# Output projection: gates and turns of rows 0 and 1 placed inside the mLSTM's last head, its own head in a fixed order

## The chip, the cores and the metric

One core of one Trainium2 chip runs the kernel. The metric is the device time of one launch in microseconds, median of three runs. The engines in the profile are PE (TensorE: matmuls, transposes by a matmul with the identity), DVE (VectorE), ACT (ScalarE), POOL (GpSimd) and SP, which only issues DMAs; ACT and POOL issue some DMAs too, in line with their other instructions.

## What is computed

A hybrid encoder block on x of 2048 x 1024 in float32. Its mixing part has two groups of 512 channels, an mLSTM with 4 heads in both directions and a Hyena operator; each is normalised and both go through one output projection. An MLP follows.

```python
y_m = group_rms(h_m, M_HEADS, mlstm_norm_w)        # h_m = (h_fwd + h_bwd) * o_gate
...
z = cv[..., OFF_HX2:OFF_HX2 + H_WIDTH] * two_sided_fft_conv(z, filt[:, 0, 1], filt[:, 1, 1], fb[1])
y_h = group_rms(z, H_GROUPS, hyena_norm_w)
mix = jnp.concatenate([y_m, y_h], axis=-1).astype(x.dtype) @ w_out
x = x + rms_norm(mix, norm_mix_post)
hm = rms_norm(x, norm_mlp_pre)
ff = jnp.square(jax.nn.relu(hm @ w_mlp_in)) @ w_mlp_out
x = x + rms_norm(ff, norm_mlp_post)
```

## The kernel before

The stages run one after the other with overlaps: input projection beside the filters, Hyena's long convolution, the mLSTM, the output projection, the MLP.

**Who orders what.** Tile pools hand out buffers by tag; a scheduler puts the instructions of each engine into one fixed order, by the order of the program and by when it reckons that operands and buffers are there. Inside `tc.manual_schedule(engines=...)` the engines named keep the order in which the code emits; where such a region falls among instructions from outside, and the order of engines not named (SP and POOL here), stay the scheduler's. On the chip each engine goes through its order and waits where something isn't ready. A DMA issued by ACT stands in ACT's order.

**The mLSTM** (`mlstm`, line 881) counts n from 0 to 68: 4 heads of 16 chunks. At each n `scores` (PE scores, ACT Exp on the mask tile mb) runs for chunk n, `values` (line 999) for chunk n - 5, and `issue` runs what values left for later: ACT's scalings into nm, DVE's sums, and for every fourth chunk the quotients (DVE's reciprocal into den, then on POOL the product nm and the sum ht) and the store of ht into ym, which ACT issues (L234). At n = 50 to 59 `loads_ahead` emits the loads that the output projection needs first. At n = 61, 64 and 68 `first_gate` does row 0's gate in three steps: the product of the inverse transform's matmuls (`gated`, L1290 and L1291) with the gate data xg; its `group_norm` (Square on ACT L1295, reduction on DVE L1297, Sqrt on ACT L239, reciprocal on DVE L241, product on POOL L1300); and `turn_split` (four PE transposes L1306, ACT's high part L166, DVE's low part L169).

**The output projection** (`out_proj`, line 1319) works on 16 rows of 128 positions. Operands are split into a high and a low part, and `mm3` makes each product of three matmuls (lines 159 to 161): low x high, high x low, high x high. `part(po, e, y, k0)` does half e of the 1024 columns for four of eight k blocks, 12 matmuls. The first half of a row by k (k0 = 4) takes the Hyena group, from `gate` and `turned`; the second (k0 = 0) the mLSTM group, from `mixed` (loads of ym and the gate o, a POOL product L1371, group_norm) and `turned`. `weight(k)` makes the parts of block k: ACT's high (L1342), DVE's low (L1343). Ahead of the loop over rows `out_proj` is not in a manual region: weights 4 to 7 with gate 1, row 0's first half, row 1's turn and first half, row 0's mixed operand, weights 0 to 3. The loop (L1455) is a manual region for PE, DVE and ACT for each i; at i it turns row i + 1's Hyena operand, does row i's first half, gate i + 3, row i + 1's mixed turn, and row i's second half. Tag xg has two buffers for gate data and o together, tag tp three PSUM banks for gates and turns, tag po three and tag h1 two for the sums.

Of the kernel before, what the change touches and what calls it, by code (L numbers as in the profile page):

```python
# [147 lines left out]
class Builder:  # L148
# [95 lines left out]
    def build(self):  # L244
        tc, nc = self.tc, self.nc
        with ExitStack() as c:
# [57 lines left out]
            self.ahead["y"] = [op.tile([128, 4, 128], F32R, name=f"y0{e}") for e in range(2)]  # L304
# [11 lines left out]
            for _ in range(6):  # L316
                next(out)
# [563 lines left out]
    def mlstm(self):  # L881
        LAG, AHEAD = 5, 10
        LOADS = {1: "v1", 5: "q1", 9: "k2", 14: "v2", 19: "q2", 32: "k3", 32 + LAG: "v3", 40: "q3"}
        self.later = []
# [6 lines left out]
        for n in range(64 + LAG):  # L891
# [19 lines left out]
            if 50 <= n < 60:  # L911
                self.loads_ahead(n - 50)
            if n in (61, 64, 64 + LAG - 1):
                self.first_gate((61, 64, 64 + LAG - 1).index(n))
# [354 lines left out]
    def loads_ahead(self, i):  # L1269

        ahead, tile = self.ahead, self.mearly.tile
        if i == 0:
            self.gate_loads(0, *ahead["gate", 0])
        elif i < 5:
            self.load(ahead[3 + i], self.io["w_out"][128 * (3 + i):128 * (4 + i), :])
        elif i == 5:
# [4 lines left out]
            t = tile([128, 3, 512], F32, tag="v", name="rda")  # L1281
            ahead["gate", 1] = t[:, 0:2], t[:, 2]
            self.gate_loads(1, *ahead["gate", 1])
# [25 lines left out]
    def first_gate(self, step):  # L1309

        (rd, xg), y = self.ahead["gate", 0], self.ahead["y"]
# [7 lines left out]
    def out_proj(self, c):  # L1319
# [24 lines left out]

        def gate(h):
            if h == 1:
                rd, xg = ahead.pop(("gate", 1))
            else:
                rd = scratch("rd").rearrange("p (r c) -> p r c", r=2)
                xg = wk.tile([128, 512], F32, tag="xg", name="xg", bufs=2)  # L1350
                self.gate_loads(h, rd, xg)
# [14 lines left out]
        def mixed(h):  # L1366
            yt = wk.tile([128, 512], F32, tag="ym", name="ymt")
            ot = wk.tile([128, 512], F32, tag="xg", name="ot", bufs=2)
            for dst, ap in ((yt, self.ym), (ot, self.vo[:, 512:1024])):
                self.load(dst, self.rows(ap, h))  # L1370
            pool.tensor_tensor(yt, yt, ot, ALU.mult)  # L1371
# [3 lines left out]
        def part(po, e, y, k0):  # L1375
            cs = slice(512 * e, 512 * e + 512)
            for k in range(4):
# [55 lines left out]
        zs, pos, yz = {}, {}, {0: ahead["y"]}  # L1433
        for k in (4, 5, 6, 7):
            weight(k)
            if k == 5:
                zs[1] = gate(1)
            yield
        pos[0] = banks(0)
        for e in range(2):  # L1440
            part(pos[0], e, yz[0], 4)
        yield
        yz[1] = turned(zs.pop(1), 1, 0)
        pos[1] = banks(1)
# [3 lines left out]
        for k in range(4):  # L1448
            weight(k)
# [5 lines left out]
        for i in range(18):  # L1455
            with tc.manual_schedule(engines={mybir.EngineType.PE,mybir.EngineType.DVE,mybir.EngineType.Activation}):
# [17 lines left out]
                if 0 < i < 16:  # L1474
# [4 lines left out]
                    if i > 1:  # L1479
                        part(pos[i], 1, yz[i], 4)  # L1480
# [486 lines left out]
```

## Time and profile before

| | us |
|---|---|
| median of 3 runs | 2704.43 (2702.84 to 2706.27) |
| profiled execution | 2700.58 |
| its span | 2698.5 |
| PE busy | 2598.6 |
| DVE busy | 1541.0 |
| ACT busy | 1230.1 |
| POOL busy | 1206.1 |

The change lies between about 1140 and 1230 us of the span. In a timeline each row has start, duration, engine, line, operation, output and input tiles, shape and count; in brackets the engine's idle time in front of it and who ended it. Matmul ends are modelled, so the distance between starts is the better measure. In a table of stretches, the granted clock of PE (PEclk) is 1.00 at 2.4 GHz and 0.50 at 1.2 GHz.

### The profile page before, as it was taken

How to read it: one execution, taken by the hardware profiler on the slowest of the kernel's cores; microseconds unless marked ns; L12 is line 12 of the kernel's file. 1: busy time of each engine (PE TensorE's matmuls, PEld its weight loads, DVE VectorE, ACT ScalarE, POOL GpSimd, SP SyncE). 2: the span in 40 equal slices, each digit the busy share in tenths (PEclk: the TensorE clock that was granted, in tenths of full speed). 3: DMA queues.
4: the chain of work that ended last, by engine and by line, in shares of the span. 5: the costliest groups of instructions: out<-in, count | busy, mean ns of one | idle time of the engine just before them, and what ended most of it. 6: DMA issues, size and time to landing. Idle time of an engine off the chain costs nothing.

```text
span 2698.5 us, 35390 instructions
## 1 busy us (share of the span) xinstructions
PE 2598.6 (96%) x12237; PEld 2109.2 (78%) x12237; DVE 1541.0 (57%) x2454; ACT 1230.1 (46%) x2292; POOL 1206.1 (45%) x964
## 2 busy tenths in 40 slices
PE   6999999999999998879997999999999999999998
PEld 4778888777798888757774788868888888888876
DVE  5676653777556666656556444474444433543477
ACT  6355544555544446643334444454544333232344
POOL 1211114555225543456667877687772340301232
PEclk9999999999999999899999999999999999999999
DMA  6233336666676658546755444555447453445555
GB/s 173 56 93 110 113 117 216 187 196 187 198 237 180 197 167 272 183 152 213 245 186 210 156 141 163 185 190 172 144 156 282 146 181 98 129 144 160 183 168 214
DMA packets 288354, 465.74 MB, mean 173 GB/s; under 512 B 37542, under 2 KB 149414, under 8 KB 287152
## 3 DMA queue, kind: packets, MB, share of 16 engines
q1 hardware_dynamic: 227600, 324.85, 39.0%
q10 hardware_dynamic: 53264, 117.53, 11.4%
q0 software_dynamic: 7312, 21.11, 3.1%
q8 instruction: 97, 1.59, 0.2%
q14 instruction: 81, 0.66, 0.1%
HBM read 289.27 MB, written 174.13 MB: 172 GB/s over the span
## 4 chain that ended last, share of the span: by engine, by line
PE 39%; DVE 4%; POOL 4%; issue 3%; DMA 2%; ACT 2%; ACTq 0%; DVEq 0%; SPq 0%; POOLq 0%
PE pm L159 13%; PE pm L160 13%; PE pm L161 13%; DMA m<-in_w_mlp_out_dram 1%; POOL xt L1255 1%; DVE cb L169 1%; POOL cb L169 1%; ACT xo L1395 1%; DVE hm L1892 0%; DVE hm L169 0%; DVE xo L1398 0%; DMA hm<-ht 0%; DVE gss L1297 0%; POOL ht L1430 0%; DVE hm L1822 0%
## 5 line engine op out<-in xcount | busy, mean ns | idle before, releaser
L166 ACT CAST cb<-m 128x1024 fp32r<-128x1024 f32 (+1 forms) x342 | 277.4, 846 | 441.3 <-PE pm L159 386.2
L169 DVE TENSOR_TENSOR cb<-m,cb 128x1024 fp32r<-128x1024 f32 (+1 forms) x222 | 237.3, 1106 | 303.1 <-ACT cb L166 302.6
L160 PE MATMUL pm<-cb 128*128 128x512 f32 x880 | 343.4, 390 | 7.8 <-DVE cb L169 7.8
L159 PE MATMUL pm<-cb 128*128 128x512 f32 x880 | 342.3, 389 | 1.3 <-DVE cb L169 1.0
L159 PE MATMUL pm<-hm,cb 128*128 128x512 f32 x840 | 331.4, 394 | 12.3 <-DVE m L1703 6.4
L161 PE MATMUL pm<-cb 128*128 128x512 f32 x880 | 342.5, 389 | 0.0
L160 PE MATMUL pm<-hm,cb 128*128 128x512 f32 x840 | 330.2, 393 | 2.5 <-POOL hm L169 2.5
L161 PE MATMUL pm<-hm,cb 128*128 128x512 f32 x840 | 329.7, 393 | 0.0
L169 POOL TENSOR_TENSOR cb<-m,cb 128x1024 fp32r<-128x1024 f32 x120 | 266.1, 2230 | 57.5 <-ACT cb L166 57.5
L1703 DVE TENSOR_TENSOR m<-pm,m 128x512 f32<-128x512 f32 x224 | 153.9, 690 | 229.4 <-PE pm L161 220.5
L159 PE MATMUL pt<-hn,w 128*128 128x512 f32 x640 | 269.5, 421 | 1.0 <-ACT hn L486 0.9
L160 PE MATMUL pt<-hn,w 128*128 128x512 f32 x640 | 253.9, 397 | 0.7 <-DVE hn L487 0.7
L161 PE MATMUL pt<-hn,w 128*128 128x512 f32 x640 | 253.0, 395 | 0.0
L169 POOL TENSOR_TENSOR raw<-raw,hi 128x512 fp32r<-128x512 f32 x160 | 206.1, 1301 | 99.7 <-ACT hi L166 74.8
L160 PEld LDWEIGHTS pm<-cb 128*128 128x128 f32 x880 | 165.2, 188 | 45.7 <-DVE cb L169 11.7
L159 PEld LDWEIGHTS pm<-hm,cb 128*128 128x128 f32 x840 | 159.2, 189 | 49.0 <-POOL cb L169 7.6
L159 PEld LDWEIGHTS pm<-cb 128*128 128x128 f32 x880 | 165.1, 188 | 36.5 <-ACT junk L1877 1.4
L161 PEld LDWEIGHTS pm<-cb 128*128 128x128 f32 x880 | 165.2, 188 | 33.9
L160 PEld LDWEIGHTS pm<-hm,cb 128*128 128x128 f32 x840 | 159.4, 190 | 37.4 <-POOL hm L169 2.9
L161 PEld LDWEIGHTS pm<-hm,cb 128*128 128x128 f32 x840 | 159.2, 190 | 34.2
L1707 ACT ACTIVATE m<-m 128x512 f32<-128x512 f32 x128 | 80.7, 630 | 229.1 <-DVE m L1703 221.7
L635 POOL DMA_DIRECT2D vp<-vst x96 | 61.2, 642 | 231.7 <-ACT vst L631 230.6
(320 smaller groups left out, 5725.6 us busy)
## 6 DMA issues: line engine op xcount, KB each, us to landing
ga<-m ACTq DMA_DIRECT2D x96, 512.0 KB, 3.6
m<-ga SPq DMA_DIRECT2D x96, 512.0 KB, 3.8
d<-st ACTq DMA_DIRECT2D x64, 512.0 KB, 3.2
m<-in_w_mlp_in_dram SPq DMA_DIRECT2D x64, 512.0 KB, 5.7
m<-in_w_mlp_out_dram SPq DMA_DIRECT2D x114, 256.0 KB, 4.0
raw<-d SPq DMA_DIRECT2D x96, 256.0 KB, 2.9
xt<-in_x_dram SPq DMA_DIRECT2D x32, 512.0 KB, 3.9
dk<-kst SPq DMA_DIRECT2D x32, 512.0 KB, 4.0
```

The lines of the kernel that those rows point to most:

```text
L159: pe.matmul(ps, w[1], x[0], start=first, stop=False)
L160: pe.matmul(ps, w[0], x[1], start=False, stop=False)
L161: pe.matmul(ps, w[0], x[0], start=False, stop=last)
L166: self.act.copy(hi, src)
L169: (eng_lo or self.dve).tensor_tensor(lo, src, hi.bitcast(F32), ALU.subtract)
L635: pool.dma_start(dst[:, 8 * b + e:8 * b + 8:2, cc:cc + 128], st[64 * e:64 * e + 64])
L1255: eng.tensor_tensor(res[:, cs], tmp[e], res[:, cs], ALU.add)
L1395: act.activation(x1, xt, AF.Square, accum_out=ss1[:, h:h + 1])
L1703: dve.tensor_tensor(dst, a, b, ALU.add)
L1707: act.activation(g, g, AF.Relu)
```

## The change

Row 1 gets operand tiles of its own, and its gate data are loaded right behind row 0's. `loads_ahead` starts at n = 40 instead of 50. Six steps of `first_gate` for rows 0 and 1 come at n = 50, 52, 54, 56, 58 and 60. The head of `out_proj` becomes one manual region for PE, DVE and ACT: gate 2's and row 0's mixed loads are emitted first; weights 4 to 7 follow, each with the 12 matmuls of rows 0 and 1 that use it; gate 2 stands behind weight 5; then weights 0 and 1, row 2's turn into row 0's tiles, weights 2 and 3, row 2's first half (its banks from h1 and tp), row 0's mixed operand. In the loop gate 2, row 2's first turn and its first half are gone from i = 0, 1 and 2.

```diff
@@ -301,7 +301,7 @@
             op = self.op = late.enter_context(tc.tile_pool(name="opre", bufs=1, side="right", reuse_waits="tile"))
             self.ahead = {k: op.tile([128, D], F32, name=f"wf{k}") for k in range(4, 8)}
             self.ahead["gate", 0] = op.tile([128, 2, 512], F32, name="rd0"), op.tile([128, 512], F32, name="xg0")
-            self.ahead["y"] = [op.tile([128, 4, 128], F32R, name=f"y0{e}") for e in range(2)]
+            self.ahead["y"] = [[op.tile([128, 4, 128], F32R, name=f"y{r}{e}") for e in range(2)] for r in range(2)]
             self.mtail = late.enter_context(tc.tile_pool(name="mtail", bufs=2, side="right", reuse_waits="tile"))
             self.mwk = ms.enter_context(tc.tile_pool(name="mwk", bufs=2, reuse_waits="tile"))
             self.mps = ms.enter_context(tc.tile_pool(name="mps", bufs=5, space=PSUM, reuse_waits="tile"))
@@ -313,8 +313,7 @@
             self.hq = c.enter_context(tc.tile_pool(name="hmq", bufs=1, reuse_waits="tile"))
             self.hm_pool = {i: self.hq for i in range(3, 8)}
             out = self.out_proj(oc)
-            for _ in range(6):
-                next(out)
+            next(out)
             late.close()
             early.close()
             hp = c.enter_context(tc.tile_pool(name="hmp", bufs=1, side="right", reuse_waits="tile"))
@@ -881,6 +880,7 @@
     def mlstm(self):
         LAG, AHEAD = 5, 10
         LOADS = {1: "v1", 5: "q1", 9: "k2", 14: "v2", 19: "q2", 32: "k3", 32 + LAG: "v3", 40: "q3"}
+        GATES = {50: (0, 0), 52: (0, 1), 54: (1, 0), 56: (1, 1), 58: (0, 2), 60: (1, 2)}
         self.later = []
         for ready in range(AHEAD // 4):
             self.weights(0, ready)
@@ -908,10 +908,10 @@
                 self.state_step(h + 1, steps[1])
             if n in LOADS:
                 self.head_loads(int(LOADS[n][1]), LOADS[n][0])
-            if 50 <= n < 60:
-                self.loads_ahead(n - 50)
-            if n in (61, 64, 64 + LAG - 1):
-                self.first_gate((61, 64, 64 + LAG - 1).index(n))
+            if 40 <= n < 50:
+                self.loads_ahead(n - 40)
+            if n in GATES:
+                self.first_gate(*GATES[n])
             self.issue(n)
 
         for n in range(64 + LAG, 64 + LAG + 5):
@@ -1271,6 +1271,9 @@
         ahead, tile = self.ahead, self.mearly.tile
         if i == 0:
             self.gate_loads(0, *ahead["gate", 0])
+            t = tile([128, 3, 512], F32, tag="v", name="rda")
+            ahead["gate", 1] = t[:, 0:2], t[:, 2]
+            self.gate_loads(1, *ahead["gate", 1])
         elif i < 5:
             self.load(ahead[3 + i], self.io["w_out"][128 * (3 + i):128 * (4 + i), :])
         elif i == 5:
@@ -1278,9 +1281,6 @@
             for k, tag in ((0, "k"), (2, "q")):
                 t = tile([128, 2, D], F32, tag=tag, name="wfa")
                 ahead[k], ahead[k + 1] = t[:, 0], t[:, 1]
-            t = tile([128, 3, 512], F32, tag="v", name="rda")
-            ahead["gate", 1] = t[:, 0:2], t[:, 2]
-            self.gate_loads(1, *ahead["gate", 1])
         else:
             self.load(ahead[i - 6], self.io["w_out"][128 * (i - 6):128 * (i - 5), :])
 
@@ -1306,9 +1306,9 @@
             self.pe.transpose(pt[:, q, :], src[:, 128 * q:128 * q + 128], self.eye)
         self.split(y[0], y[1], pt)
 
-    def first_gate(self, step):
-
-        (rd, xg), y = self.ahead["gate", 0], self.ahead["y"]
+    def first_gate(self, r, step):
+
+        (rd, xg), y = self.ahead["gate", r], self.ahead["y"][r]
         if step == 0:
             self.gated(self.op, self.mps.tile([128, 512], F32, tag="m", name="py"), rd, xg, xg)
         elif step == 1:
@@ -1342,13 +1342,16 @@
             act.activation(wo[0][k], wf, AF.Copy, scale=yw[:, k:k + 1])
             dve.scalar_tensor_tensor(wo[1][k], wf, yw[:, k:k + 1], wo[0][k].bitcast(F32), ALU.mult, ALU.subtract)
 
+        opened = {}
+
+        def opening(h):
+            rd = scratch("rd").rearrange("p (r c) -> p r c", r=2)
+            xg = wk.tile([128, 512], F32, tag="xg", name="xg", bufs=2)
+            self.gate_loads(h, rd, xg)
+            return rd, xg
+
         def gate(h):
-            if h == 1:
-                rd, xg = ahead.pop(("gate", 1))
-            else:
-                rd = scratch("rd").rearrange("p (r c) -> p r c", r=2)
-                xg = wk.tile([128, 512], F32, tag="xg", name="xg", bufs=2)
-                self.gate_loads(h, rd, xg)
+            rd, xg = opened.pop(h, None) or opening(h)
             zt = wk.tile([128, 512], F32, tag="yz", name="yz", bufs=3)
             self.gated(wk, ps.tile([128, 512], F32, tag="tp", name="py", bufs=3), rd, xg, zt)
             self.group_norm(wk, zt, xg, 64)
@@ -1363,18 +1366,22 @@
             self.turn_split(ps.tile([128, 512], F32, tag="tp", name="ptp", bufs=3), src, y)
             return y
 
-        def mixed(h):
+        def mixed_loads(h):
             yt = wk.tile([128, 512], F32, tag="ym", name="ymt")
             ot = wk.tile([128, 512], F32, tag="xg", name="ot", bufs=2)
             for dst, ap in ((yt, self.ym), (ot, self.vo[:, 512:1024])):
                 self.load(dst, self.rows(ap, h))
+            return yt, ot
+
+        def mixed(h, tiles=None):
+            yt, ot = tiles or mixed_loads(h)
             pool.tensor_tensor(yt, yt, ot, ALU.mult)
             self.group_norm(wk, yt, ot, 128)
             return yt
 
-        def part(po, e, y, k0):
+        def part(po, e, y, k0, ks=range(4)):
             cs = slice(512 * e, 512 * e + 512)
-            for k in range(4):
+            for k in ks:
                 self.mm3(po[e], (y[0][:, k, :], y[1][:, k, :]), (wo[0][k0 + k][:, cs], wo[1][k0 + k][:, cs]),
                          k0 == 4 and k == 0, k0 == 0 and k == 3)
 
@@ -1430,25 +1437,31 @@
                 pool.dma_start(self.ht[h // 8, i - 1][:, :, 128 * t:128 * t + 128], src)
 
         turned_even = {}
-        zs, pos, yz = {}, {}, {0: ahead["y"]}
-        for k in (4, 5, 6, 7):
-            weight(k)
-            if k == 5:
-                zs[1] = gate(1)
-            yield
-        pos[0] = banks(0)
-        for e in range(2):
-            part(pos[0], e, yz[0], 4)
-        yield
-        yz[1] = turned(zs.pop(1), 1, 0)
-        pos[1] = banks(1)
-        part(pos[1], 0, yz[1], 4)
-        part(pos[1], 1, yz[1], 4)
-        ym = {0: turned(mixed(0), 0, 1)}
-        for k in range(4):
-            weight(k)
-        yield
-        ys = {}
+        zs, pos, yz, ys = {}, {}, dict(enumerate(ahead["y"])), {}
+
+        with tc.manual_schedule(engines={mybir.EngineType.PE,mybir.EngineType.DVE,mybir.EngineType.Activation}):
+            opened[2] = opening(2)
+            tiles = mixed_loads(0)
+            pos[0], pos[1] = banks(0), banks(1)
+            for k in (4, 5, 6, 7):
+                weight(k)
+                for i in range(2):
+                    for e in range(2):
+                        part(pos[i], e, yz[i], 4, (k - 4,))
+                if k == 5:
+                    zs[2] = gate(2)
+            for k in range(2):
+                weight(k)
+
+            yz[2] = yz[0]
+            self.turn_split(ps.tile([128, 512], F32, tag="tp", name="ptp", bufs=3), zs.pop(2), yz[2])
+            for k in range(2, 4):
+                weight(k)
+            pos[2] = [self.h1p.tile([128, 512], F32, tag="h1", name="po1"), ps.tile([128, 512], F32, tag="tp", name="po2", bufs=3)]
+            for e in range(2):
+                part(pos[2], e, yz[2], 4)
+            ym = {0: turned(mixed(0, tiles), 0, 1)}
+        yield
         self.load(wb, io["norm_mix_post"].partition_broadcast(128))
         xns = {}
         wl = c.enter_context(tc.tile_pool(name="owl", bufs=2, side="right", reuse_waits="tile"))
@@ -1456,14 +1469,13 @@
             with tc.manual_schedule(engines={mybir.EngineType.PE,mybir.EngineType.DVE,mybir.EngineType.Activation}):
                 if i == 0:
                     ys[1] = mixed(1)
-                    zs[2] = gate(2)
                     part(pos[0], 0, ym[0], 0)
                     ym[1] = turned(ys.pop(1), 1, 1)
                     zs[3] = gate(3)
                     ys[2] = mixed(2)
-                if 0 < i < 15:
+                if 1 < i < 15:
                     yz[i + 1] = turned(zs.pop(i + 1), i + 1, 0)
-                if 1 < i < 16:
+                if 2 < i < 16:
                     pos[i] = banks(i)
                     part(pos[i], 0, yz[i], 4)
                 if 0 < i < 15:
@@ -1476,7 +1488,7 @@
                     part(pos[i], 0, ym[i], 0)
                     if i + 2 < 16:
                         ys[i + 2] = mixed(i + 2)
-                    if i > 1:
+                    if i > 2:
                         part(pos[i], 1, yz[i], 4)
                 if 2 <= i:
                     turn_out(i - 2, xns.pop(i - 2))
```

## Rows read from the trace of the kernel before

**Rows 1.** The page: PE's busy time, share and instructions; and its busy tenths in 40 slices of the span.
```profile
PE 2598.6 (96%) x12237; PEld 2109.2 (78%) x12237; DVE 1541.0 (57%) x2454; ACT 1230.1 (46%) x2292; POOL 1206.1 (45%) x964
...
PE   6999999999999998879997999999999999999998
```

**Rows 2.** Busy time of each engine by stretch (us; in brackets the instructions), PE's granted clock, DMA share and GB/s.
```profile
1167.43:1181.44 14.01, 9.37 (x35) 6.58 (x34) 11.38 (x14) 9.21 (x12) 7.10 (x5) 0.88 0.72 221
...
1181.44:1194.16 12.72, 8.51 (x29) 6.78 (x29) 5.56 (x8) 3.15 (x6) 6.10 (x4) 0.73 0.54 171
...
1228.31:1242.92 14.61, 14.61 (x71) 11.39 (x70) 7.85 (x16) 6.34 (x17) 7.90 (x8) 1.00 0.64 201
```

**Rows 3.** Timeline of ACT, 1140 to 1166 us.
```profile
1144.64 0.69 ACT L993 ACTIVATE mb<-mb,qt 128x128 f32<-128x128 f32 x2 [1.25 <-POOL mb L980]
...
1150.40 0.63 ACT L1015 ACTIVATE nm<-ps,qt 128x129 f32<-128x129 f32 x2 [2.89 <-POOL ht L1030]
...
1153.26 0.43 ACT L993 ACTIVATE mb<-mb,qt 128x128 f32<-128x128 f32 x1
...
1157.08 0.89 ACT L1015 ACTIVATE nm<-ps,qt 128x129 f32<-128x129 f32 x3 [2.00 <-POOL ht L1030]
...
1158.63 0.63 ACT L1015 ACTIVATE nm<-ps,qt 128x129 f32<-128x129 f32 x2 [0.67 <-PE ps L1008]
...
1162.44 1.14 ACT L1015 ACTIVATE nm<-ps,qt 128x129 f32<-128x129 f32 x4 [2.39 <-POOL ht L1030]
...
1163.60 1.28 ACT L239 ACT_TABLE_LOAD   x1
...
1164.90 0.30 ACT L239 ACTIVATE gr_sd<-gss,eps 128x8 f32<-128x8 f32 x1
```

**Rows 4.** Timeline of POOL, 1140 to 1176 us.
```profile
1145.16 3.75 POOL L1028 TENSOR_TENSOR nm<-nm,den 128x1024 f32<-128x1024 f32 x2
...
1148.87 2.14 POOL L1030 TENSOR_TENSOR ht<-nm 128x512 f32<-128x512 f32 x2
...
1153.57 1.90 POOL L1028 TENSOR_TENSOR nm<-nm,den 128x1024 f32<-128x1024 f32 x1 [2.56 <-DVE den L1026]
...
1166.68 1.04 POOL L1300 TENSOR_TENSOR xg<-xg,gr_r 128x512 f32<-128x512 f32 x1
...
1173.14 1.95 POOL L1030 TENSOR_TENSOR ht<-nm 128x512 f32<-128x512 f32 x1
```

**Rows 5.** Timeline of all engines, 1150 to 1201 us: PE's rows where it had waited, and the turn of row 1.
```profile
1172.32 0.71 PE L159 MATMUL po<-wo,y 128*128 128x512 f32 x2 [3.03 <-DVE y L169]
...
1174.29 0.76 PE L160 MATMUL po<-wo,y 128*128 128x512 f32 x1 [1.26 <-DVE wo L1343]
...
1180.84 0.60 PE L1306 MATMUL ptp<-eye,yz 128*128 128x128 f32 x4
...
1185.65 0.80 PE L159 MATMUL po<-wo,yt 128*128 128x512 f32 x1 [4.21 <-DVE yt L169]
```

**Rows 6.** Timelines of ACT and of DVE, 1163 to 1182 us: weights.
```profile
1169.81 1.15 ACT L1342 ACTIVATE wo<-wf,yw 128x1024 fp32r<-128x1024 f32 x1
...
1175.54 2.19 ACT L1342 ACTIVATE wo<-wf,yw 128x1024 fp32r<-128x1024 f32 x2 [2.54 <-POOL ht L1030]
...
1176.73 1.29 DVE L1343 SCALAR_TENSOR_TENSOR wo<-wf,yw,wo 128x1024 fp32r<-128x1024 f32 x1
...
1179.23 2.07 DVE L1343 SCALAR_TENSOR_TENSOR wo<-wfa,yw,wo 128x1024 fp32r<-128x1024 f32 x1
```

**Rows 7.** Stretches as in rows 2, cut where the granted clock changes.
```profile
1174.30:1177.00 2.70, 2.70 (x7) 2.12 (x8) 2.70 (x3) 1.46 (x2) 0.80 (x1) 0.50 1.01 359
...
1185.60:1190.50 4.90, 4.85 (x11) 3.80 (x12) 3.22 (x5) 1.20 (x4) 3.03 (x2) 0.50 0.48 155
```

**Rows 8.** Timeline of all engines, 1150 to 1225 us: loads, turns, gate 3, halves.
```profile
1168.79 1.10 SPq L231 DMA_DIRECT2D rd<-d  x2
...
1181.76 3.08 POOL L1371 TENSOR_TENSOR ymt<-ymt,ot 128x512 f32<-128x512 f32 x2 [1.55 <-DMA ymt<-ym]
...
1193.72 0.60 PE L1306 MATMUL ptp<-eye,ymt 128*128 128x128 f32 x4
...
1195.72 0.55 PE L159 MATMUL po<-wo,yt 128*128 128x512 f32 x1
...
1198.67 0.60 PE L1306 MATMUL ptp<-eye,ymt 128*128 128x128 f32 x4
...
1199.10 1.88 PE L1290 MATMUL py<-rd,s1i 128*128 128x512 f32 x4
...
1199.92 0.69 DVE L169 TENSOR_TENSOR yt<-ptp,yt 128x512 fp32r<-128x512 f32 x1 [1.15 <-ACT yt L166]
...
1203.18 0.30 ACT L239 ACTIVATE gr_sd<-gss,eps 128x8 f32<-128x8 f32 x1 [0.75 <-DVE gss L1297]
...
1203.61 0.60 PE L1306 MATMUL ptp<-eye,yz 128*128 128x128 f32 x4
...
1206.82 0.66 PE L1306 MATMUL ptp<-eye,ymt 128*128 128x128 f32 x4 [0.89 <-POOL ymt L1300]
...
1212.88 0.60 PE L1306 MATMUL ptp<-eye,yz 128*128 128x128 f32 x4
...
1218.23 0.65 PE L1306 MATMUL ptp<-eye,ymt 128*128 128x128 f32 x4 [0.25 <-POOL ymt L1300]
```

## The prediction, made before the changed kernel ran

> **What bounds the kernel now.** The page gives PE 96% of the span, with a dip in its busy slices near the middle [rows 1], so the reading goes by stretch. From 1228 us on, one row of the output projection takes 14.6 us and PE is busy for all of it at full clock [rows 2]; after that the busy slices of PE are full to the end [rows 1]. So whatever is lost or won before row 3's first half begins, at 1228.31 us, is carried to the end nearly unchanged, and that moment is my mark. In front of it PE is busy 9.4 of 14.0 us, then 8.5 of 12.7 [rows 2]. Read next whom PE waited for there: 3.03 us for row 0's low part, 1.26 us for the first low weight, 4.21 us for row 1's low part [rows 5]. After those holes the granted clock is 0.50, that is 1.2 GHz, from 1174.3 to 1177.0 and again from 1185.6 to 1190.5 [rows 7]. Last, read ACT and POOL ahead of 1167 us: in the mLSTM's closing groups ACT stands behind its own store, which waits for POOL's sum: 2.89, 2.00 and 2.39 us [rows 3], and POOL waits 2.56 us for DVE's reciprocal [rows 4].
>
> **Part 1, gates and turns of rows 0 and 1 inside the last head.** A gate's four fp32 matmul records (1.7 us of PE from start to start), its product, Square, reduction, Sqrt, reciprocal and POOL product, then four transposes, a cast and a subtraction are the same instructions as before. Row 0's move some 12 us earlier, row 1's from behind the mLSTM to inside it. Added are table switches. Exps run from 1144.6 to 1153.7 us and the first Sqrt only at 1164.9, behind one table load of 1.28 us [rows 3]. Steps 52 and 56 now put two Sqrts where those last eight Exps run, so the order can become Exp, Sqrt, Exp, Sqrt, Exp and, in the head, Sqrt: up to four loads more, 4 x 1.28 = 5.1 us of ACT, or none if all Exps happen to go first. I count all four and two Sqrts of 0.3: 5.7 us of ACT between 1143 and 1156; ACT's waits behind the stores there (2.89 and 2.00) hide about 4.1 of it, and 1.6 us are left. POOL is busy without a break from 1145.2 to 1151.0 [rows 4]; gate 0's product there (1.04 us) adds 1.0, gate 1's falls into the 2.56 us that POOL then waits. Against that, gate 0's product leaves 1166.68, where it holds back a sum and its store by 1.04 [rows 4], and its matmuls leave the place where ACT waited 0.67 us for PE [rows 3]: -1.7. Sum for the end of the mLSTM: +0.9 us. Bounds: -1.7 (every addition hidden) and +5 (the loads hidden nowhere).
>
> The Trainium skill ("ScalarE: Activation LUTs", What ACT_TABLE_LOAD costs) puts a switch at a load of 1.28 us plus a drain of 1.38 us, and advises finishing one table set before the next; it speaks against this part. By the page four switches would be 10.6 us, an estimate from it, instead of 5.1. The trace shows the load alone: ACT's scalings end at 1163.58, the load starts at 1163.60 and the Sqrt at 1164.90 [rows 3].
>
> **Part 2, the head in a fixed order**, put on the old clock with the mLSTM's end unchanged:
> - Weight 4: ACT starts it at 1169.81 and takes 1.15 [rows 6]; it writes where mLSTM tiles lay, so I leave it there. DVE, which had row 1's product and row 0's subtraction first, can now follow at once, but POOL's last sum runs until 1175.1 [rows 4], and a low weight beside POOL's work took 2.07 instead of 1.29 us [rows 6]. So it is there at 1173.1, where PE's steady run used to begin at 1174.29 [rows 5]: 1.2 us gained. That rows 0 and 1 are ready brings no more, since the weights are not.
> - Weights 4 and 5 for two rows, 24 matmuls, as many as row 0 alone needed: 22 of them took 6.55 us, from 1174.29 to 1180.84, with a cold stretch [rows 5]. PE's hole in front is no shorter now, so I take 6.8: 1179.9.
> - Gate 2 stands here, between weights 5 and 6, in a fixed order on PE, DVE and ACT. Its loads, at 1168.8 before [rows 8], are in time. Its matmuls end at 1181.8. ACT's Square waits for DVE's product, the Sqrt for DVE's reduction, and queued behind them on ACT is weight 6, for which PE waits. In the loop, from the end of gate 3's matmuls (1199.10 + 1.88) to the end of its Sqrt (1203.48) it is 2.5 us [rows 8]; then 1.15 for the high and 1.29 for the low weight [rows 6]: PE has weight 6 whole at 1186.8. **The old hole of 4.2 us is closed and one of 5.0 us opens**, and the clock falls to 0.50 again, as after 1185.6 [rows 7].
> - Weights 6 and 7, 24 matmuls behind such a hole: 8.07 us before, from 1185.65 to 1193.72 [rows 5, 8]; one of them precedes the low weight, so 7.7: 1194.5.
> - Row 2's turn: transposes, cast, subtraction, with nothing else for PE: 1.94 us, as from 1198.67 to 1200.61 [rows 8]: 1196.4. Its 24 matmuls take 5.65 (6.06 from 1206.82 to 1212.88, less a turn's transposes of 0.4 [rows 8]): 1202.1.
> - Row 0's second operand was loaded and multiplied by 1184.8 [rows 8]; behind weights 2 and 3 on ACT and DVE its norm ends near 1201.5, just covered. Its turn is bare, 1.94: 1204.0. Before, gate 2's matmuls lay beside it.
> - Row 0's second half, row 1's turn and gate 3, unchanged: 7.89 us (1195.72 to 1203.61) [rows 8]: 1211.9.
> - Row 1's second half, 1203.61 to 1212.88 before. Row 2's first turn is gone from it, yet row 2's second turn came 7.72 us after gate 3's matmuls began (1199.10 to 1206.82). They now begin at 1207.4, so 1215.1, and 6.06 more [rows 8]: 1221.2.
> - Row 2 has lost the 24 first-half matmuls that covered the loop's latency. Row 3's turn and gate 5 end at 1223.3, but the next turn came 14.62 us after row 0's last matmul (1203.61 to 1218.23) [rows 8]: now 1226.5, a hole of 3.2 us, of which I am least sure. From that turn to the mark it was 10.1 us [rows 2, 8], less 12 matmuls of 2.8: 1233.8.
>
> Against 1228.31 that is +5.5 us; without the last hole +2.3. With part 1's +0.9: **+6.4**. PE's work is the same. Saved are two turns and half a gate behind the mLSTM (1.7 us) and the old holes; opened are one of 5.0 at gate 2 and four of 1.4, 1.5, 1.3 and 3.2, because matmuls that covered turns were pulled forward. No transfer is added; row 1's gate loads and two head loads change places on SP's queue, ahead of need by tens of us in the one case and of about 3 us in the other, so they cost nothing unless gate 2's rows land after 1179.9.
>
> The profiled execution took 2700.58 us (span 2698.5), 3.85 below the median of 2704.43. The sum gives 2707.0 on its scale and 2710.8 on the median's; rounded, I forecast 2710.0. A measurement of this kernel can tell some 0.2%, 5.4 us, from no change, so the forecast stands at that edge.
>
> **Rivals.**
> 1. The closing mLSTM groups shrink. Decided by where each store falls on ACT: gate 0's Square, Sqrt and POOL product leave the last groups, and if the store then comes after the next group's scalings, ACT's waits of 2.9, 2.0 and 2.4 us go. For: POOL needs only 2.95 us for a group [rows 4] and a group takes 5.4 to 6.7 [rows 3]. Against: POOL's work hangs on the same scalings. Price -7.3 - 1.7 = -9 instead of +0.9: 2700.9, not slower; with the hole of 3.2 absent too, 2697.7.
> 2. The end of the mLSTM moves out by the whole of the table loads. Decided by whether both Sqrts come while POOL waits for ACT, not ACT for POOL. +5 instead of +0.9: 2714.9. By the skill's drain (same page and section) four times 1.38 would come on top, 2720, an estimate; the row above speaks against it.
> 3. The change doesn't do what it says: the gates get their bank late, rows 0 and 1 are turned only at the end, and PE begins at 1174.3 as before. The rest stands and 1.2 are lost: 2712.
>
> **How the numbers follow.** Forecast 0.47, rival 1 0.32, rival 2 0.13, rival 3 0.08. The forecast's own range is 2704 to 2714: 0.25 slower by over 0.2%, 0.20 within, 0.02 faster. Rival 1 is faster by over 0.2% with 0.18 and within with 0.14, rival 2 slower, rival 3 half slower and half within. Sum: faster 0.20, same 0.38, slower 0.42. The range for 8 in 10 takes in most of rivals 1 and 2: 2698 to 2717.
>
> **What would show it.** Right: PE idle some 5 us behind gate 2's matmuls, ended by weight 6, then clock 0.50; bare turns of 1.4 us before row 2's and row 0's halves; more than one table load between 1140 and 1170. Wrong: weight 6 on ACT ahead of gate 2's Square, the last store of ym well before 1175, or row 3's first half before 1228.

## The result and the profile after

Five runs of the changed kernel gave 2714.43 to 2718.41 us, median 2716.55, against 2704.43: the ratio is 1.0041 (95% interval 1.0028 to 1.0053), 0.4% or 12 us slower. The profiled execution took 2718.41 us (span 2716.5), the slowest of the five; that of before was a low one of its own (2700.58). So spans can't simply be subtracted: after's trace is 4.4 us behind already at the mLSTM's first scores (1038.45 against 1034.02), where nothing has changed. From here on places are given in us since those first scores, so that this offset drops out; rows of the profile keep the time of their own span.

Three landmarks: the mLSTM's last value matmul ends at 133.4 before and 139.1 after; the last store of ym is issued at 141.1 and 146.2; row 3's first half, the prediction's mark, begins at 194.3 and 205.5. The end of the mLSTM is 5.7 us later, and the way from there to the mark is 66.4 us instead of 60.9, 5.5 longer.

PE's timeline of the changed kernel from the last values to the mark, the rows ahead of which it had waited and those that bound the stretches between:
```profile
1178.81 0.50 PE L159 MATMUL po<-wo,y 128*128 128x512 f32 x1 [1.31 <-DVE den L1025]
1180.89 0.51 PE L160 MATMUL po<-wo,y 128*128 128x512 f32 x1 [1.58 <-DVE wo L1343]
...
1187.91 1.88 PE L1290 MATMUL py<-rd,s1i 128*128 128x512 f32 x4
1193.89 0.49 PE L159 MATMUL po<-wo,y 128*128 128x512 f32 x1 [4.10 <-ACT wo L1342]
1195.29 0.80 PE L160 MATMUL po<-wo,y 128*128 128x512 f32 x1 [0.90 <-DVE wo L1343]
...
1202.16 0.60 PE L1306 MATMUL ptp<-eye,yz 128*128 128x128 f32 x4
1204.16 0.50 PE L159 MATMUL po<-wo,y 128*128 128x512 f32 x1 [1.40 <-DVE y L169]
1211.87 0.50 PE L159 MATMUL po<-wo,yt 128*128 128x512 f32 x1 [1.40 <-DVE yt L169]
1222.61 0.66 PE L1306 MATMUL ptp<-eye,ymt 128*128 128x128 f32 x4 [1.02 <-POOL ymt L1300]
1234.93 0.66 PE L1306 MATMUL ptp<-eye,ymt 128*128 128x128 f32 x4 [3.90 <-POOL ymt L1300]
```
Read it against [rows 5, 8]. The 3.03 us for row 0's low part and the 4.21 for row 1's are gone. In their place stand 4.10 and 0.90 behind gate 2's matmuls, both ended by weight 6, then 1.40, 1.40, 1.02 and 3.90. The stretches by engine say the same in one number: busy time of PE, PEld, DVE, ACT and POOL, clock, DMA share and GB/s, from the last values to the mark. First before, then the same kernel in a second execution (run c0, below), then after:
```profile
1167.43:1228.31 60.88, 50.90 (x207) 37.38 (x207) 35.01 (x59) 27.23 (x54) 28.85 (x23) 0.92 0.62 192
```
```profile
1170.43:1230.45 60.02, 51.43 (x208) 37.57 (x207) 35.06 (x59) 27.31 (x54) 29.00 (x23) 0.91 0.60 194
```
```profile
1177.51:1243.91 66.40, 50.79 (x196) 36.84 (x197) 32.61 (x54) 26.61 (x50) 28.22 (x22) 0.92 0.54 176
```
PE is busy 51 us in all three, so what differs is waiting: 10.0 and 8.6 us before, 15.6 after. Row 1's gate and turn have left this stretch (196 records instead of 207), yet PE's busy time is the same: behind the holes a matmul of a first half takes 0.63 us, later 0.40.

ACT's timeline of the changed kernel, the function-table loads and the scalar steps beside them, as [rows 3]:
```profile
1151.25 1.28 ACT L239 ACT_TABLE_LOAD   x1
1152.54 0.30 ACT L239 ACTIVATE gr_sd<-gss,eps 128x8 f32<-128x8 f32 x1
...
1158.24 1.28 ACT L993 ACT_TABLE_LOAD   x1 [2.69 <-POOL ht L1030]
...
1162.03 1.28 ACT L239 ACT_TABLE_LOAD   x1
...
1168.60 1.28 ACT L993 ACT_TABLE_LOAD   x1
...
1190.55 0.63 ACT L1295 ACTIVATE xg<-yz 128x512 f32<-128x512 f32 x1 [9.21 <-DVE yz L1291]
1191.20 1.28 ACT L239 ACT_TABLE_LOAD   x1
1192.50 0.30 ACT L239 ACTIVATE gr_sd<-gss,eps 128x8 f32<-128x8 f32 x1
1192.70 2.17 ACT L1342 ACTIVATE wo<-wf,yw 128x1024 fp32r<-128x1024 f32 x2
```
Sqrt, Exp, Sqrt, Exp and in the head Sqrt: five loads where one was, the order that the prediction counted. The last four rows are the hole behind gate 2: weights 6 and 7 (the last row) stand on ACT behind gate 2's Square, a table load and its Sqrt.

### The profile page after: what moved, and what is told of

Its sections match the earlier page's. It is cut to its first block, busy times and chain, and to the rows that moved or that the text cites. A ratio compares the mean times of both kernels' runs of the same rounds, so it can differ in the third digit from the quotient of the medians.

```text
span 2716.5 us, 35390 instructions
## 1 busy us (share of the span) xinstructions
PE 2602.5 (96%) x12237; PEld 2110.8 (78%) x12237; DVE 1537.1 (57%) x2454; ACT 1236.2 (46%) x2296; POOL 1204.4 (44%) x964
## 4 chain that ended last, share of the span: by engine, by line
PE 51%; DMA 6%; DVE 5%; POOL 5%; issue 3%; ACT 3%; ACTq 0%; SPq 0%; DVEq 0%; POOLq 0%
PE pm L159 13%; PE pm L160 13%; PE pm L161 13%; PE pt L160 2%; PE pt L159 2%; PE pt L161 2%; PE pi L1177 1%; DMA mb<-mrow 1%; POOL xt L1255 1%; DMA hm<-ht 1%; DVE cb L169 1%; DMA v<-vo 1%; DMA m<-in_w_mlp_out_dram 1%; ACT xo L1402 1%; PE pv L966 1%
## 5 line engine op out<-in xcount | busy, mean ns | idle before, releaser
L159 PEld LDWEIGHTS pm<-cb 128*128 128x128 f32 x880 | 165.1, 188 | 35.8 <-ACT junk L1889 1.4
```

The lines of the kernel that those rows point to most:

```text
L159: pe.matmul(ps, w[1], x[0], start=first, stop=False)
```

## The experiments

Eleven runs follow, c0 being the kernel before once more. All of them are on one scale here, in us since the mLSTM's first scores; the last column is the ratio to the kernel before, with its interval. "Clock" is PE's granted clock from 100 us to the last values. "Not busy" is the stretch less PE's busy time in it.

| kernel | last values | clock | last store of ym | row 0's second turn | mark | last values to mark (PE not busy) | ratio |
|---|---|---|---|---|---|---|---|
| before | 133.4 | 1.00 | 141.1 | 159.7 | 194.3 | 60.9 (10.0) | |
| c0: before again | 134.9 | 0.92 | 142.6 | 160.3 | 194.9 | 60.0 (8.6) | |
| after | 139.1 | 0.93 | 146.2 | 171.4 | 205.5 | 66.4 (15.6) | 1.0041 [1.0028, 1.0053] |
| e1: part 1 alone | 139.6 | 0.93 | 146.8 | 160.7 | 196.7 | 57.1 (8.5) | 1.0007 [0.9999, 1.0016] |
| e2: gates late | 138.9 | 0.92 | 144.6 | 175.3 | 209.9 | 71.0 (17.6) | 1.0048 [1.0033, 1.0063] |
| e3: no Sqrt in the mLSTM | 137.0 | 1.00 | 146.0 | 172.0 | 206.0 | 69.0 (16.9) | 1.0046 [1.0033, 1.0059] |
| e4: weights before gate 2 | 138.4 | 0.93 | 145.5 | 170.1 | 205.2 | 66.8 (16.0) | 1.0045 [1.0031, 1.0059] |
| e5: row 2 in the loop | 139.3 | 0.93 | 146.4 | 167.0 | 201.6 | 62.3 (12.0) | 1.0031 [1.0019, 1.0042] |
| e6: e4 and e5 | 140.3 | 0.92 | 147.4 | 165.1 | 201.7 | 61.5 (12.3) | 1.0022 [1.0013, 1.0031] |
| e13: after, only row 0 gated ahead | 133.7 | 1.00 | 140.9 | 165.7 | 200.7 | 67.0 (15.4) | 1.0026 [1.0017, 1.0035] |
| e14: part 2 alone | 134.6 | 0.92 | 144.5 | 168.2 | 202.2 | 67.6 (16.3) | 1.0045 [1.0032, 1.0058] |
| e15: before, row 0 early | 133.2 | 1.00 | 140.4 | 154.7 | 189.8 | 56.7 (5.8) | 0.9984 [0.9974, 0.9993] |
| e16: e15, row 1 first | 133.6 | 0.97 | 140.8 | 155.2 | 190.3 | 56.7 (5.7) | 0.9990 [0.9981, 0.9999] |

**The two parts, each by itself.** e1 has the changed mLSTM with the head and loop of before; e14 the mLSTM of before with the changed head.
```diff
 # e1: head and loop of before, with both rows turned already
-zs, pos, yz = {}, {}, {0: ahead["y"]}
+zs, pos, yz = {}, {}, dict(enumerate(ahead["y"]))
 ...
-    if k == 5:
-        zs[1] = gate(1)
 ...
-yz[1] = turned(zs.pop(1), 1, 0)
 # e14: from after
-GATES = {50: (0, 0), 52: (0, 1), 54: (1, 0), 56: (1, 1), 58: (0, 2), 60: (1, 2)}
+GATES = {61: (0, 0), 64: (0, 1), 68: (0, 2)}
-yz = dict(enumerate(ahead["y"]))
+yz = {0: ahead["y"][0], 1: ahead["y"][0]}
```


> Part 1 alone: the six gate and turn steps stay inside the last head at n = 50 to 60, the projection's head and loop are those of before (row 1's gate and turn gone from the head). My reading: the end of the mLSTM stays late by the 5.7 us that it was late in the changed kernel (1177.5 less the 4.4 us that its run was late before the mLSTM began, against 1167.4); the head has no hole for row 1's turn (4.2 us idle, some 2 us of half clock behind it) and three pieces of work less (1.7 us). Sum about 5.7 - 6 = 0: 2702 to 2707, within 0.2% of before. Rival, that the end of the mLSTM was late only because the fixed head's instructions were mixed into it: then part 1 alone gains those 6 us, 2698.

Measured: 2706.59 us, 1.0007, no change that can be told. The mLSTM ends as late as in the changed kernel (139.6), but the old head makes up for most of it: 57.1 us to the mark instead of 60.9, with row 1's gate and turn gone from it. Its one long hole is a new one of 4.3 us, at row 0's second turn.

> Part 2 alone: the mLSTM of the kernel before (row 0's gate at steps 61, 64 and 68), with the head of the changed kernel; row 1's first half takes row 0's operand, so row 1's gate and turn are left out. Theory that the two parts each have their own price, which add: the head's own 5.5 us are left, 2711 (2709 to 2713). Rival that the head loses only because it starts late, and made up its work otherwise: 2704 to 2707. Rival that the head's price is larger than its 5.5 us (part 1 alone came to 1 us of 12): 2714 to 2717.

Measured: 2716.43 us, 1.0045, as slow as the whole change. The expectation of 5.5 us is refuted, and the rival with the larger price (2714 to 2717) came out. Whether the two parts add can't be told: the ratios give 1.0052 against the change's 1.0041, within their intervals, and the marks 1.8 to 2.4 and 7.3 to 7.9 us against 10.6 to 11.2. The mLSTM's last values come at 134.6, between the two executions of before, and from there the head takes 67.6 us, although row 1's gate and turn are left out of it: 6.7 to 7.6 more than before. Its last store is 1.9 to 3.4 us later than before, because on DVE two low weights of the head stand among the steps of the last quotients, as they don't in the change:
```profile
1174.90 1.28 DVE L1343 SCALAR_TENSOR_TENSOR wo<-wf,yw,wo 128x1024 fp32r<-128x1024 f32 x1
...
1176.18 1.28 DVE L1343 SCALAR_TENSOR_TENSOR wo<-wf,yw,wo 128x1024 fp32r<-128x1024 f32 x1
1177.38 0.20 DVE L1026 RECIPROCAL den<-den 128x8 f32<-128x8 f32 x1
```
The cleanest pair for the head is after and e1, whose mLSTMs end within 0.5 us of each other: there the fixed head takes 66.4 us and the old one 57.1, so it costs 9.3. In the change, part 1 takes a gate and a turn off the head, and loses that again at the mLSTM's end.

**The table loads.** e2 moves the gates later, their Sqrts behind the last Exps; e3 puts Square in place of Sqrt in the two gates inside the mLSTM.
```diff
 # e2
-GATES = {50: (0, 0), 52: (0, 1), 54: (1, 0), 56: (1, 1), 58: (0, 2), 60: (1, 2)}
+GATES = {61: (0, 0), 62: (1, 0), 64: (0, 1), 65: (1, 1), 67: (0, 2), 68: (1, 2)}
 # e3, in rstd, where func is AF.Sqrt unless the caller names another
-self.act.activation(sd, ss, AF.Sqrt, scale=1.0 / n, bias=self.eps)
+self.act.activation(sd, ss, func, scale=1.0 / n, bias=self.eps)
 # e3, in first_gate
-self.group_norm(self.op, xg, rd[:, 0, :], 64)
+self.group_norm(self.op, xg, rd[:, 0, :], 64, AF.Square)
```


> The changed kernel with the six steps moved behind the last Exp: n = 61, 62, 64, 65, 67, 68 in place of 50 to 60. One table load is left ahead of the head instead of four. If the loads are what the mLSTM's end pays (4 more x 1.28 = 5.1 us), the time falls by 3 to 5 us, to 2712 to 2713, less up to 2 us that the steps cost in the last groups; the holes in the head stay at 5, 1.4, 1.4, 1 and 4 us. Rival, that the gates' matmuls and POOL products cost it, wherever they stand: 2716 as before, or more, since they now meet the last groups.

> The changed kernel with Square in place of Sqrt in the norm of rows 0 and 1's gates, the same instruction count and sizes, no other place touched; rows 0 and 1 are then normalised wrongly. No table switch is left inside the mLSTM. My reading: four loads go and with them 4 to 5.5 us: 2711 to 2712.5. Rival, that ACT would have stood behind POOL's sums for that time anyway: 2715 to 2716.5, and the end of the mLSTM no earlier.

Measured: 2717.92 (1.0048) and 2717.05 us (1.0046). With one load instead of four (e2), or none (e3), the time is the change's. In e3 the last values come 2.1 us earlier than after, at a granted clock of 1.00 instead of 0.93 ahead of them, but the last store does not (146.0 against 146.2), nor does the mark. The stretch from 100 us to the last store, in the order of columns above, after and then e3:
```profile
1138.45:1184.66 46.21, 38.51 (x210) 31.50 (x209) 30.09 (x69) 28.06 (x73) 25.85 (x18) 0.91 0.27 82
```
```profile
1137.30:1183.30 46.00, 36.65 (x213) 29.89 (x213) 30.21 (x71) 23.38 (x73) 25.91 (x18) 0.94 0.29 90
```
Without the loads ACT is busy 4.7 us less and idle 4.5 us more in a stretch of the same length: the loads lie where ACT would otherwise have stood idle. Which of its waits they filled is not shown, for these differ between two executions of one kernel. For POOL's sum ACT's scalings wait (in all, times, longest, over the same 48 us) in the first execution of before and in the second:
```profile
ACT nm L1015 <- POOL ht L1030: 7.7, 4, 2.9
```
```profile
ACT nm L1015 <- POOL ht L1030: 3.3, 2, 2.9
```
My reading after the result, that the loads cost the mLSTM its 5 us, fell with this run. e2 adds that late gates are no way out: row 1's cast then stands on ACT behind a store that waits for POOL's sum, weight 4 behind the cast, and PE begins the head 4.8 us after the last values. ACT's timeline of e2:
```profile
1178.62 0.58 ACT L166 CAST y<-pty 128x512 fp32r<-128x512 f32 x1 [2.81 <-POOL ht L1030]
1179.10 2.19 ACT L1342 ACTIVATE wo<-wf,yw 128x1024 fp32r<-128x1024 f32 x2
```

**One gate or two.** e13 is the changed kernel with row 0's gate and turn alone. Row 0's norm is called at n = 54 instead of the change's 52, but its Square and Sqrt run at the same places, 110.8 and 113.8 us (after: 111.1 and 114.1).

> The changed kernel without row 1's gate and turn: row 1's first half takes row 0's operand, so row 1's gate and turn are left out; row 0's stay at steps 50, 54 and 58. Theory that the second gate's instructions are what moves the end of the mLSTM: last store of ym 141 us after the last head's first scores, as before (the change: 146), and a time within 1.5 us of the next run. Theory that the early place among the last Exps does it, whatever the number of gates: last store at 145 or later, and 3 to 5 us longer than the next run.

(The 141, 145 and 146 us in it count from the mLSTM's first scores, not from the last head's, and "the next run" is e14.) Measured: last values at 133.7, last store at 140.9, as before. So the early place costs nothing, though a Sqrt still lies among the Exps there; it is the second gate that moves the end of the mLSTM. From e13 to after it moves by 5.4 us at the last values and 5.3 at the last store, but not all of that is the gate's: PE's granted clock differs too, and it differs as much between the two executions of before. The stretch from 100 us to the last values, in the order of columns above, for before, c0, after, e13 and e3:
```profile
1134.02:1167.43 33.41, 29.02 (x185) 24.28 (x183) 21.53 (x58) 19.08 (x62) 18.60 (x14) 1.00 0.19 56
```
```profile
1135.57:1170.43 34.86, 31.97 (x189) 27.11 (x187) 22.03 (x58) 19.66 (x62) 18.62 (x14) 0.92 0.18 53
```
```profile
1138.45:1177.51 39.06, 34.24 (x199) 28.33 (x197) 24.82 (x63) 25.67 (x71) 18.89 (x15) 0.93 0.16 48
```
```profile
1134.89:1168.60 33.71, 30.32 (x194) 25.15 (x192) 23.78 (x61) 22.09 (x69) 17.85 (x14) 1.00 0.21 55
```
```profile
1137.30:1174.30 37.00, 32.09 (x203) 26.61 (x202) 25.15 (x65) 20.93 (x70) 19.15 (x15) 1.00 0.17 50
```
Sorted by clock, all runs agree. At 1.00 the last values come at 133.2 to 133.7 with one gate in the mLSTM (before, e13, e15) and at 137.0 with two (e3, which has no Sqrt there). At 0.97 they come at 133.6 with one (e16). At 0.92 to 0.93 they come at 134.6 and 134.9 with one (e14, c0) and at 138.4 to 140.3 with two (after, e1, e2, e4, e5, e6). So at like clock the second gate costs 3.3 to 5.7 us there, 4.2 between c0 and the change. Two of the four loads went with it, but by e3 those explain at most 2.1 us at the last values and 0.2 at the last store. Which of the second gate's steps (matmuls, product, Square, reduction, POOL product, cast, subtraction) holds the groups up was not separated. The time, 2712.64 us, is some 4 below e14's, not within the 1.5 expected. 1.5 of it lie ahead of the mark: row 0's operand is also there earlier (PE begins the head at 135.0 against 138.6).

**The holes of the head.** e4 calls weights 6 and 7 ahead of gate 2; e5 puts row 2's turn and first half back into the loop; e6 does both.
```diff
 # e4
 for k in (4, 5, 6, 7):
     weight(k)
+for k in (4, 5, 6, 7):
     for i in range(2):
 # e5
-yz[2] = yz[0]
-self.turn_split(ps.tile([128, 512], F32, tag="tp", name="ptp", bufs=3), zs.pop(2), yz[2])
 ...
-pos[2] = [...]
-for e in range(2):
-    part(pos[2], e, yz[2], 4)
 ...
-    if 1 < i < 15:
+    if 0 < i < 15:
-    if 2 < i < 16:
+    if 1 < i < 16:
 ...
-    if i > 2:
+    if i > 1:
```


> The changed kernel with weights 4 to 7 emitted ahead of the matmuls and of gate 2, so that on ACT and DVE weight 6 no longer stands behind gate 2's Square and Sqrt; PE's order is the same. My reading: the hole of 5.0 us behind gate 2's matmuls goes and with it the half clock behind it (24 matmuls took 7.0 instead of 5.6 us): -6.4 us, less about 1 us of a new wait at row 2's turn: 2710 to 2711. Rival, that weights 6 and 7 are late anyway or that row 2's turn only takes the wait over: 2714 to 2716.

Measured: 2718.52 us (1.0045), nothing won. Weight 6 came at once, and PE stood 1.5 us ahead of row 2's turn and 5.3 behind it instead, as the rival has it. ACT's and POOL's timelines of e4 show why:
```profile
1197.60 0.63 ACT L1295 ACTIVATE ot<-ymt 128x512 f32<-128x512 f32 x1 [5.72 <-POOL ymt L1378]
1198.13 0.57 ACT L166 CAST y<-ptp 128x512 fp32r<-128x512 f32 x1
```
```profile
1196.31 1.26 POOL L1378 TENSOR_TENSOR ymt<-ymt,ot 128x512 f32<-128x512 f32 x1 [2.79 <-DMA ot<-vo]
```
Row 2's cast is ready, but ACT has the Square of a mixed row in front of it, row 1's, which belongs to the loop. That Square waits for POOL's product, the product for a load of vo that was issued only at 1189.46, behind the loads of ym that wait for the last store; its buffer had been gate 2's until the reduction of gate 2's norm ended at 1188.90.

> Row 2's turn and first half go back to their places in the loop (i = 1 and 2); rows 0 and 1 stay turned inside the mLSTM, and gate 2 stays between weights 5 and 6. Theory of the prediction (row 2's pulled-forward matmuls uncover the turns behind them): of the bare waits, those at row 2's turn, row 0's second turn and the two later in the loop (1.4, 1.5, 1.3 and 3.2 us by the prediction) mostly go, the hole behind gate 2 (5 us) stays: 2711 (2709 to 2713). Rival (row 0's second operand, which starts from the last store of ym, ends last anyway): a new hole of 4 us or more stands before row 0's second turn, and the time is 2714 to 2718.

> As the run before it (row 2's turn and first half back in the loop), and weights 6 and 7 ahead of gate 2 as well. Theory of the prediction: the hole behind gate 2 goes too, what is left is what the gates do inside the mLSTM: 2706 to 2708, as with part 1 alone (2706.6). Rival (each removed wait only makes room for the next, as with the weights alone): PE waits some 4 to 5 us for row 0's second operand, weights 2 and 3 or gate 3 come late, and the time stays at 2712 to 2718.

Measured: 2712.12 us (1.0031) and 2711.51 (1.0022). e5 is the number of the prediction's theory: the 1.4 us at row 2's turn and the last hole of 3.9 go, PE is not busy for 12.0 us instead of 15.6, and the mark comes 3.9 earlier. (2.2 of that are left where the MLP begins.) Row 0's second turn keeps its 1.4 us and gets 1.0 in front. e6 shows its rival's mechanism, at a time between the two: the hole behind gate 2 is gone and one of 6.9 us stands at row 0's second turn. All engines' timeline of e6, the step that ended it and what fed that:
```profile
1194.10 1.35 POOL L1378 TENSOR_TENSOR ymt<-ymt,ot 128x512 f32<-128x512 f32 x1 [2.06 <-DMA ot<-vo]
1194.75 1.36 ACT L1295 ACTIVATE ot<-ymt 128x512 f32<-128x512 f32 x2
...
1200.17 1.11 PE L1306 MATMUL ptp<-eye,ymt 128*128 128x128 f32 x4 [6.88 <-POOL ymt L1300]
```
ACT ran weights 6, 7 and 0 to 3 first, and both mixed rows' Squares behind them.

**The spread, and a better version.** c0 is the kernel before once more. e15 is the kernel before with row 0's gate and turn at steps 50, 54 and 58 and the loads ahead at 40 to 49; e16 also calls row 1's gate ahead of weight 4 and its turn ahead of weight 6.
```diff
 # e15, on the kernel before
-if 50 <= n < 60:
-    self.loads_ahead(n - 50)
-if n in (61, 64, 64 + LAG - 1):
-    self.first_gate((61, 64, 64 + LAG - 1).index(n))
+if 40 <= n < 50:
+    self.loads_ahead(n - 40)
+if n in (50, 54, 58):
+    self.first_gate((50, 54, 58).index(n))
```


> The kernel before once more, for one look at how far its stages vary from one execution to the next. If what the changed kernel lost behind row 3's first half (3 to 4 us, most of it where the MLP begins) is its own, this profile repeats the old one: the MLP's first 100 matmuls in 48.6 us. If it is only the spread of executions, they take 50 us or more here, and the span is near 2703.

Measured: span 2703.9 us, 5.4 longer than the first profile of the same kernel. 1.6 of it lie ahead of the mLSTM's first scores, 3.2 behind the mark, most of that at the MLP's beginning: its first 100 matmuls in 51.4 us instead of 48.5, the changed kernel's in 51.8. The stretches, in the order of columns above (first profile of before, then c0, then after):
```profile
1416.46:1464.99 48.53, 38.41 (x117) 21.84 (x116) 36.70 (x33) 23.01 (x33) 34.41 (x21) 0.93 0.57 214
```
```profile
1418.70:1470.10 51.40, 41.27 (x118) 22.83 (x117) 36.20 (x33) 23.00 (x33) 32.37 (x21) 0.87 0.55 206
```
```profile
1430.87:1482.62 51.75, 41.60 (x117) 23.01 (x116) 35.21 (x34) 23.00 (x33) 33.11 (x21) 0.87 0.55 206
```
So what the change seemed to lose behind the mark is the spread of executions. Against the two marks of before, 194.3 and 194.9, its own 205.5 is 11 us late: nearly all of the 12.

> The kernel before with one thing of the change: row 0's gate and turn at steps 50, 54 and 58 and the loads ahead ten steps earlier; row 1 and the head as before. Theory (the first halves' gain is given back at row 1's cast, which ACT has queued behind the Square of a mixed row that hangs on the last store of ym): PE's steady run in the head begins some 3 us sooner after the last values (3.4 against 6.9), the hole of 4.2 us in front of row 1's low part grows by as much, and the time is the same, 2704 to 2707. Rival (the hole does not grow): 2701 to 2703. Rival of the prediction's table loads: 2708 or more.

> As the run before it, and in the head, still in no fixed order, row 1's gate is called ahead of weight 4 and its turn ahead of weight 6, so that its cast need not stand behind a mixed row's Square. Theory: the hole of 4.2 us in front of row 1's first half goes, PE next waits for row 0's second turn, which can come 14 us behind the last store of ym (as with part 1 alone) and not 18.6: 3 to 4 us faster than before, 2701 to 2703. Rival (row 1's chain ahead of the weights makes weights 6 and 7 late): 2706 to 2710.

Measured: 2703.01 us (0.9984) and 2703.17 (0.9990), both a little faster than before, with intervals that end below 1, and some 14 us faster than the changed kernel. The theory for e15 is refuted: PE did have the first low weight 3.4 us after the last values, but the hole in front of row 1 is gone instead of growing; what PE waits for on the way are weights (1.2, 1.2 and 1.9 us). PE's timeline of e15, the first rows of row 1's first half and of row 0's second half, then ACT's, before and e15:
```profile
1182.36 0.49 PE L159 MATMUL po<-wo,yt 128*128 128x512 f32 x1
...
1190.73 0.51 PE L159 MATMUL po<-wo,yt 128*128 128x512 f32 x1 [0.36 <-DVE yt L169]
```
```profile
1183.64 0.63 ACT L1295 ACTIVATE ot<-ymt 128x512 f32<-128x512 f32 x1 [2.60 <-POOL ymt L1371]
1184.18 0.57 ACT L166 CAST yt<-ptp 128x512 fp32r<-128x512 f32 x1
```
```profile
1180.99 0.59 ACT L166 CAST yt<-ptp 128x512 fp32r<-128x512 f32 x1 [1.50 <-PE ptp L1306]
1182.29 0.63 ACT L1295 ACTIVATE ot<-ymt 128x512 f32<-128x512 f32 x1 [0.71 <-POOL ymt L1371]
```
Before, row 1's cast stood behind the Square that waits for the chain from the last store, the same wait as in e4. In e15 the order in which the program is laid out came out the other way round, so the cast no longer waits. e16, made to force that, found it done already and adds nothing.

## Why the prediction came out as it did

**Direction and size.** Forecast 2710.0, measured 2716.55: slower, as the likeliest case had it, inside the range of 2698 to 2717 but only just, and outside the forecast's own 2704 to 2714.

**Part 2 was right to the tenth, by errors that cancel, which is luck.** Predicted +5.5 us from the last values to the mark; measured 66.4 - 60.9 = +5.5, or +6.4 against the second execution of before. The holes came one by one: 5.0 us behind gate 2, measured 4.10 + 0.90, ended by weight 6 behind gate 2's Sqrt; 1.4 at row 2's turn, 1.40; 1.5 at row 0's, 1.40; 1.3 at row 2's second turn, 1.02; 3.2 at row 3's, 3.90. Off were the start and the tail. The steady run began 3.4 us after the last values, not the 5.7 that follow from 1173.1 (before: 6.9 [rows 5]); I had left weight 4 where it was, 2.4 us after the last values, and ACT scales it 0.1 us after them. And from the last of these turns to the mark it took 9.0 us, not 7.3: behind that hole 12 matmuls took 4.4 us at a granted clock of 0.62 (1235.3 to 1239.8 us), as against 3.0 in the loop before. With the mLSTM's end really unchanged, as the sum assumes, e14's head costs 6.7 to 7.6.

**Part 1 is the step that was mis-sized.** Predicted +0.9 us at the mLSTM's end, measured +5.7, or +4.2 against the second execution of before, whose granted clock ahead of it (0.92) is close to the change's (0.93); that is 3.3 to 4.8 of the 5.8 us by which the sum, 2710.8, fell short. The mechanism that I priced was the wrong one. The order of Exps and Sqrts, the four more loads and ACT's idle time hiding them all came as written, and e3 shows that the loads cost the last store nothing. What I let pass at next to nothing was the second gate: I gave gate 0's POOL product 1.0 us, laid gate 1's into one wait of POOL of 2.56, counted a Sqrt of 0.3 for each, and gave the rest of the chain no price. By the runs at like clock gate 1's chain costs 3.3 to 5.7. I treated a group of the mLSTM as having slack because single engines had some; the second gate's steps pass through all four engines, in order on each. That this is how they hold up the groups is my reading; no run separates the steps.

**A premise was read too widely.** [rows 1] do not show PE full from the mark to the end: the slice from 1417 to 1484 us, where the MLP begins, stands at 7 tenths. It is there that two executions of before differ by 2.9 us (c0).

**Rival 2** named nearly the right time (2714.9) for the wrong reason: the end did move by 4 to 6 us, but not by the loads, which were hidden. The Trainium skill ("ScalarE: Activation LUTs", What ACT_TABLE_LOAD costs) would have added a drain of 1.38 us to each load. The trace differs: a load of 1.28 us starts at 1151.25 and its Sqrt at 1152.54, so no drain behind it shows. **Rival 1** is refuted: the closing groups did not shrink, the last store comes at 146.2 and not ahead of 141. **Rival 3** did not occur: rows 0 and 1 were ready, and PE waited for weights.

**Where the expected gain went.** It is there in e13 and e15: with row 0 turned early PE begins the head at 135.0 or 134.5 instead of 138.3. In the change the second gate takes it back ahead of the head, and then the fixed order spends it: gate 2 in front of weight 6, and row 2's matmuls taken from the places where they covered turns. Removing one of these waits shows the next (e4, e6), because row 0's second operand hangs on the last store of ym through a load, two products and a norm, and on ACT it shares its place with the Square of row 1, whose load waits for a buffer that gate 2 still holds. From that store to the turn it takes 25.2 us after, 17.6 in e6, 13.9 in e1 and 14.3 in e15.

What stays open: which step of the second gate delays the mLSTM's groups, why the granted clock in the mLSTM's last stretch is 1.00 in some executions and 0.92 in others, and how much of e15's gain comes from the early gate itself and how much from the order on ACT that came with it.

## What to carry to other kernels

Matmuls pulled forward into a hole are taken from a place where they covered something: add up PE's idle time over a fixed stretch, to the point from which PE is full, not only the hole that closes. In front of an instruction that waits for a long chain, look at what is queued behind it on the same engine: here a Square or a Sqrt held up the weight or the cast for which PE stood, before the change and after it. And a step that passes through four engines is not free because each of them has slack somewhere; test it by leaving it out, and compare stretches that ran at the same granted clock, for which the baseline needs a second profile.

## What was not expected of the hardware

Five table loads of 1.28 us where one had been cost nothing that reached the end: the time with one load or none in the mLSTM was within 0.1% of the change's. And one and the same kernel ran the mLSTM's last stretch (from 100 us to the last values) at a granted clock of 1.00 in one execution and 0.92 in the next, 33.4 against 34.9 us, and the MLP's first stretch at 0.93 and 0.87, 48.5 against 51.4 us; the second alone is over half of the 5.4 us by which its two spans differ.
